# A hybrid decoder block: two VectorE operations of a recurrence step done for both heads at once, with another stage order and other buffer counts

## The chip, the cores and the metric

The kernel runs on one core of a Trainium2 chip. The core has five engines with queues of their own, which meet through semaphores: TensorE (PE in the profile; its weight loads are PEld), VectorE (DVE), ScalarE (ACT), GpSimd (POOL) and SyncE (SP), which issues most of the DMA transfers. The metric is the device time of one execution in microseconds (us).

## The reference, cut to what matters

The reference is one layer on 2048 tokens of width 1024, in float32. After an RMS norm one input projection feeds two groups of four heads, each head 128 wide. Their outputs, gated, go through one output projection and are added to the input. Then come a norm, a gated MLP (width 2816) with a causal convolution of width 3, a second addition and a last norm. The gated-DeltaNet heads carry a state matrix per head from chunk to chunk; this is the part that the change edits:

```
def step(state, inp):
    u_b, w_c, qk_c, qd_c, kd_c, cd_c = inp
    u = u_b - jnp.einsum('bhck,bhkv->bhcv', w_c, state)
    o = jnp.einsum('bhck,bhkv->bhcv', qd_c, state) + jnp.einsum('bhij,bhjv->bhiv', qk_c, u)
    state = state * cd_c[..., None, None] + jnp.einsum('bhck,bhcv->bhkv', kd_c, u)
    return state, o
```

The other four heads are retention heads: the same kind of recurrence with a fixed decay per head and rotary queries and keys.

## The kernel before

**Numbers.** Every large product is done in three passes of matmuls on split operands: each value is a high part (a rounded copy made by ScalarE) and a low part (the rest, by VectorE). `mm3` at L111 to L113 issues the three passes for channel-major and output products, L383 to L385 for token-major projections. The large products use seven multiplications in place of eight, on sums and differences of the quarters of their operands.

**Stages.** `mixers` covers everything up to the second norm, `mlp_up` the up projection and the convolution, `mlp_down` the down projection and the last norm. `mixers` works on four token blocks of 512 tokens (four chunks of 128). For each block there are items: `pro` (load and normalize x), `k0 v0 q0 kq` (retention projections, with a rotary turn L732 to L737 half on VectorE, half on GpSimd), `dec` (decays), `a0` to `a3` (one gated-DeltaNet head each: projections, convolution, transposes, Gram products), `b0 b1` (for a pair of heads, the triangular solve), `g0 g1` (the rest of the solve and the recurrence of a pair), `h0` to `h3` (retention heads), `p0 p1` (the gate projections, whose SiLU at L396 writes tiles called `mix`), `G0 G1` (gate the heads' outputs and transpose them), `W1` to `W7` (the seven products of the output projection) and `N` (residual and second norm).

**What sets the order.** The string `ORDER` names the items of all four blocks by hand, as `2k0` for item `k0` of block 2. Within it a list scheduler sets each engine's final order, interleaving the steps of several items, and each engine then runs its list strictly in order. SyncE's list holds the DMA issues, and one that must wait for its buffer holds up those behind it.

**Buffers.** On-chip tiles are slots of one size, 4 KB in each partition. A tag (`mix`, `NT`, `wvr` and so on) has an upper count in `BUFS` or in one of the N... constants, but the slots themselves are shared between tags, and the program as built fixes which slot a tile gets. So a tile can come to wait for the last reader of a quite different tile. The eight PSUM banks are shared in the same manner.

**The solve (L591 to L617).** For a pair of heads GpSimd runs 31 steps of two operations each, L603 (multiply rows of `Nb`, which a DMA brings in) and L605 (add to the rows below), about 28 us in all. Its queue also holds the rotary additions (L737), the subtractions on output-projection weights (L177) and small powers for norms (L533, L716, L812, L859).

**The recurrence (L665 to L706).** `gdn_rec` handles one chunk of a pair of heads. TensorE computes the products with the state (`ks`, L679), VectorE corrects the values (L682), TensorE applies the solved triangle (`wps`, L690), VectorE multiplies its rows by a number per row, `brk`, into `u` (L694, one operation per head), TensorE makes the state's increment and the intra-chunk output (`sps`, L698), VectorE updates the state (L700) and adds the two parts of the output (L703, one per head), and ScalarE sums the output's squares (L705). The next chunk's L679 needs the state of L700, so the four chunks of a pair are a chain; other items' matmuls fill TensorE between its links. `brk` comes from `gdn_kq` and `ss`, the squares' sums of L523, and is a small tile per head.

**Output-projection weights (L154 to L199).** `load_v` brings two halves of a weight into `wvr` tiles, GpSimd forms the needed difference in a `wvt` tile (L177; product 4 takes three subtractions per weight), ScalarE makes the high part (L197) and VectorE the low part (L198) of the `wv` tile that TensorE reads. Before the next product, `done` (L855 to L860) stores finished rows and norms them, with a power on GpSimd at L859.

**MLP constants.** `NHH` counts residual tiles and `NVV` value tiles in `mlp_down`, `NACC` the convolution's accumulators in `mlp_up`.

Of the kernel before, what the change touches and what calls it, by code (L numbers as in the profile page):

```python
# [11 lines left out]
ALU = mybir.AluOpType  # L12
# [2 lines left out]

NW = 5
LA = 1
NHH = 3
NUU = 10
NVR = 4  # L20
NVV = 20
NWUR = 2
NST = 4
NUC = 7
NACC = 6
NWU = 9
NWV = 5
FX = 1
# [5 lines left out]
NLATE = 4  # L34
NXR = 7
FD = 4
BUFS = {"n1": 8, "ykq": 5, "kv": 4, "NT": 5, "AT": 6, "o": 2, "n2s": 11, "xk": 2, "og": 1, "co": 6, "Cw": 4,
        "wx": 1, "wsq": 3, "wvr": 3, "wvt": 8, "ca": 8, "mix": 6, "D": 8, "rk": 5, "rq": 4, "rv": 8, "Ar": 1,
        "Nb": 6, "rot": 1, "rrow": 7}

ORDER = ("0pro 0k0 0v0 0dec 0a0 0q0 0a1 0a2 0h0 0b0 0h1 0a3 0b1 0g0 0kq 0g1 0h2 0p1 1pro 0p0 1k0 0G0 0h3 "
# [5 lines left out]
P = 128  # L47
S = 2048
D = 1024
# [3 lines left out]
NT = TB // P  # L53
# [149 lines left out]
def mixers(ctx, tc, base, base_used, marks, drp, mm3, gamma, mhalf, n1w, n2w, gcw, gv127, epsr, gnw, n2d, hd,  # L203
           x, xT, w_kq, w_v, w_g, w_rk, w_r0, w_r, w_o, rows, masks, rot):
    nc = tc.nc
    PE, ACT, DVE, POOL = nc.tensor, nc.scalar, nc.vector, nc.gpsimd
# [113 lines left out]
    def small(nm, n=16, bufs=2):  # L320
        if nm not in ring:
            ring[nm] = [pc(bufs, n), 0, bufs]
        e = ring[nm]
        e[1] += 1
        return e[0][:, e[1] % e[2]]
# [13 lines left out]
    def A_items(b, st):  # L339
# [165 lines left out]
        def gdn_kq(h):  # L505
            def f(w):
                hd_ = st["hd", h] = {}
                ykq = hd_["ykq"] = al("ykq", (P, 2, TB))
                ss = hd_["ss"] = small("sskq", 8, 12)
                pst = []  # L510
                for i in range(2):
                    ps = chmajor(w, i)
# [4 lines left out]
                    ps = mbank("kqtr")  # L517
# [5 lines left out]
                        ACT.activation(jk, ps[:, c * P:(c + 1) * P], AF.Square,  # L523
                                       accum_out=ss[:, i * 4 + c:i * 4 + c + 1])
                DVE.tensor_scalar(ss, ss, EPS, None, op0=ALU.add)
                brk = hd_["brk"] = small("brk", 4, 8)
                nbrk = hd_["nbrk"] = small("nbrk", 4, 8)
                bh = st["beta"].rearrange("p (t h) -> p h t", h=NH)[:, h]
                DVE.reciprocal(brk, ss[:, :4])
# [5 lines left out]
                ps = pst[0]  # L535
# [8 lines left out]
                for cc in range(2):  # L544
                    ps = mbank("kk")
                    for c1 in range(2):
                        c = cc * 2 + c1
# [117 lines left out]
        def gdn_rec(hs, c):  # L665
            def f(_):
# [8 lines left out]
                n = len(hs)  # L675
# [9 lines left out]
                    ACT.activation(e["o"][:, sl], ps[:, (n + i) * P:(n + i + 1) * P], AF.Copy,  # L685
                                   scale=st["eg"][:, jj[i]:jj[i] + 1])
                ps = rbank("wps")
                us = []
                for i, e in enumerate(H):
                    PE.matmul(ps[:, i * P:(i + 1) * P], e["TT"][:, sl], e["vp"][:, sl], start=True, stop=True)  # L690
                for i, e in enumerate(H):
                    u = small("u", P, 4)
                    us.append(u)
                    DVE.tensor_scalar(u, ps[:, i * P:(i + 1) * P], e["brk"][:, c:c + 1], None, op0=ALU.mult)  # L694
                ps = rbank("sps")
                for k, w in enumerate(("kd", "A")):
                    for i, e in enumerate(H):
                        PE.matmul(ps[:, (k * n + i) * P:(k * n + i + 1) * P], e[w][:, sl], us[i], start=True, stop=True)  # L698
                for i, h in enumerate(hs):
                    DVE.scalar_tensor_tensor(Sst[h], Sst[h], st["eg"][:, 16 + jj[i]:17 + jj[i]], ps[:, i * P:(i + 1) * P],  # L700
                                             op0=ALU.mult, op1=ALU.add)
                for i, e in enumerate(H):
                    DVE.tensor_tensor(e["o"][:, sl], ps[:, (n + i) * P:(n + i + 1) * P], e["o"][:, sl], op=ALU.add)  # L703
                    jk = small("jk", P, 1)
                    ACT.activation(jk, e["o"][:, sl], AF.Square, accum_out=e["so"][:, c:c + 1])  # L705
            return f  # L706
# [572 lines left out]
```

## Time and profile before

| | |
|---|---|
| median of three runs | 2495.29 us (2495.28 to 2497.01) |
| the profiled execution | 2495.6 us |
| its span in the trace | 2493.8 us |
| mean granted TensorE clock | 0.993 |
| busy PE, VectorE, ScalarE, GpSimd | 2413.2, 1622.6, 1000.8, 574.4 us |

The profile shows one execution, in microseconds from the start of its span. A row of a timeline gives start, duration, engine, line, operation, output and inputs, size and count; what stands in brackets is how long the engine had been idle and what released it. A row of waits gives the waiting and the releasing line, then total, count and longest. A row of windows gives busy times by engine in a stretch, the clock that TensorE was granted there (1.00 is full), the busy share of the DMA engines and GB/s. In the summary, a row of digits gives tenths for 40 equal slices of the span. Ends of matmuls are modelled, so starts are the safer reading. The mixers fill about the first 1165 us, the up projection the time to about 1960, the down projection the rest.

### The profile page before, as it was taken

Reading aid. Unit: us, or ns where it says so; the run is one execution under the profiler, and the core shown is the slowest. Engines: PE = TensorE matmul, PEld = TensorE weight load, DVE = VectorE, ACT = ScalarE, POOL = GpSimd, SP = SyncE. Lnnn points to the kernel's source line nnn. Section 1 sums busy time; section 2 is a strip of 40 time slices with the busy share of each in tenths; the row PEclk is TensorE's granted clock in tenths of the full one; section 3 lists DMA queues with packets and bytes.
Section 4 is the critical chain, followed back from the end, with each engine's and each line's share of the span. In section 5 each row is a group of like instructions: output and inputs, shape, how many; then the busy total and the mean of one; then the engine's idle time right before and its main releaser. Section 6 shows DMA issues by size and latency. Waiting matters only on the chain.

```text
span 2493.8 us, 35729 instructions
## 1 busy us (share of the span) xinstructions
PE 2413.2 (97%) x12476; PEld 2019.8 (81%) x12476; DVE 1622.6 (65%) x3198; ACT 1000.8 (40%) x2151; POOL 574.4 (23%) x891
## 2 busy tenths in 40 slices
PE   8998899999999999998899999999999999999998
PEld 7877787887888878886688888888888888888887
DVE  6755766435652673536889888896565567555795
ACT  6544544434342552425464344442222224332332
POOL 1354146521046205140011000000000001422180
PEclk9999899999999999999999999999999999999999
DMA  8756498863865646644899888867676868764794
GB/s 321 254 187 245 172 320 299 294 218 121 290 217 162 216 175 228 235 166 140 331 338 347 303 296 297 297 257 279 224 259 236 288 235 278 223 216 143 242 295 133
DMA packets 285604, 609.64 MB, mean 244 GB/s; under 512 B 40880, under 2 KB 120944, under 8 KB 285424
## 3 DMA queue, kind: packets, MB, share of 16 engines
q1 hardware_dynamic: 269424, 593.69, 67.7%
q10 hardware_dynamic: 16000, 13.67, 1.8%
q8 instruction: 98, 1.61, 0.3%
q14 instruction: 82, 0.67, 0.1%
HBM read 410.56 MB, written 196.71 MB: 244 GB/s over the span
## 4 chain that ended last, share of the span: by engine, by line
PE 78%; POOL 6%; DMA 6%; DVE 5%; issue 3%; ACT 2%; SPq 0%; ACTq 0%; POOLq 0%; DVEq 0%
PE p L111 10%; PE p L112 10%; PE p L113 10%; PE d L113 5%; PE d L111 4%; PE d L112 4%; PE tok L383 4%; PE tok L385 4%; PE tok L384 4%; PE chm L111 2%; PE chm L113 2%; PE chm L112 2%; POOL pers L605 2%; POOL pers L603 2%; DMA wvr<-in_w_o 2%
## 5 line engine op out<-in xcount | busy, mean ns | idle before, releaser
L112 PE MATMUL p<-x,wu 128*128 128x512 f32 x1176 | 458.5, 390 | 5.8 <-DVE x L929 5.8
L111 PE MATMUL p<-x,wu 128*128 128x512 f32 x1176 | 453.8, 390 | 4.6 <-ACT x L928 3.0
L113 PE MATMUL p<-x,wu 128*128 128x512 f32 x1176 | 450.6, 389 | 0.0
L383 PE MATMUL tok<-wc,n 128*128 128x512 f32 (+2 forms) x768 | 274.8, 362 | 10.8 <-ACT n L371 10.2
L384 PE MATMUL tok<-wc,n 128*128 128x512 f32 (+2 forms) x768 | 275.8, 359 | 0.0
L385 PE MATMUL tok<-wc,n 128*128 128x512 f32 (+2 forms) x768 | 274.8, 361 | 0.0
L111 PEld LDWEIGHTS p<-x,wu 128*128 128x128 f32 x1176 | 220.6, 188 | 54.5 <-ACT x L928 6.1
L112 PEld LDWEIGHTS p<-x,wu 128*128 128x128 f32 x1176 | 220.8, 188 | 54.3 <-DVE x L929 9.0
L113 PEld LDWEIGHTS p<-x,wu 128*128 128x128 f32 x1176 | 220.7, 188 | 45.3
L1049 DVE SCALAR_TENSOR_TENSOR acc<-uc,base,acc 128x1022 f32<-128x1022 f32 (+1 forms) x176 | 221.2, 1279 | 40.0 <-ACT acc L1046 34.3
L1007 DVE TENSOR_TENSOR uc<-p,uc 128x512 f32<-128x512 f32 x224 | 153.3, 687 | 133.2 <-PE p L113 131.0
L177 POOL TENSOR_TENSOR vt<-vr 128x512 f32<-128x512 f32 x44 | 70.8, 1615 | 620.5 <-DMA vr<-in_w_d 444.4
L112 PE MATMUL d<-v,uu 128*128 128x512 f32 x448 | 174.3, 389 | 0.0
L113 PE MATMUL d<-v,uu 128*128 128x512 f32 x448 | 174.3, 389 | 0.0
L111 PE MATMUL d<-v,uu 128*128 128x512 f32 x448 | 174.3, 389 | 0.0
L383 PEld LDWEIGHTS tok<-wc,n 128*128 128x128 f32 x768 | 145.9, 190 | 30.4 <-ACT n L371 10.2
L384 PEld LDWEIGHTS tok<-wc,n 128*128 128x128 f32 x768 | 145.7, 190 | 19.4
L385 PEld LDWEIGHTS tok<-wc,n 128*128 128x128 f32 x768 | 144.7, 189 | 19.3
L111 PE MATMUL chm<-n,wc 128*128 128x512 f32 x384 | 151.5, 395 | 0.0
L113 PE MATMUL chm<-n,wc 128*128 128x512 f32 x384 | 151.5, 395 | 0.0
L112 PE MATMUL chm<-n,wc 128*128 128x512 f32 x384 | 151.3, 394 | 0.0
L1054 POOL COPY base<-uc 128x2 f32<-128x2 f32 x44 | 33.2, 754 | 452.9 <-DVE uc L1007 452.9
(247 smaller groups left out, 4864.3 us busy)
## 6 DMA issues: line engine op xcount, KB each, us to landing
wu<-wu SPq DMA_DIRECT2D x308, 512.0 KB, 6.0
wc<-wd SPq DMA_DIRECT2D x166, 512.0 KB, 5.1
wv<-wo SPq DMA_DIRECT2D x84, 512.0 KB, 5.4
wd<-wc SPq DMA_DIRECT2D x60, 512.0 KB, 4.6
ur<-au SPq DMA_DIRECT2D x56, 512.0 KB, 5.5
wur<-in_w_u SPq DMA_DIRECT2D x44, 512.0 KB, 6.0
au<-st SPq DMA_DIRECT2D x88, 256.0 KB, 4.8
vr<-in_w_d SPq DMA_DIRECT2D x44, 512.0 KB, 6.0
```

Of the source, the lines that this page charges most:

```text
L111: PE.matmul(ps, ah, bh, start=(first and i == 0), stop=False, skip_group_check=chk)
L112: PE.matmul(ps, ah, bl, start=False, stop=False, skip_group_check=chk)
L113: PE.matmul(ps, al, bh, start=False, stop=(i == n - 1), skip_group_check=chk)
L177: POOL.tensor_tensor(tt[:, j], a, b_, op=ALU.subtract)
L383: PE.matmul(ps, ah, wh, start=(k == 0), stop=False)
L384: PE.matmul(ps, ah, wl, start=False, stop=False)
L385: PE.matmul(ps, al_, wh, start=False, stop=(k == KT - 1))
L603: POOL.tensor_tensor(tm[:, :, :n], Nb[:, j:j + 1, j + 1:].to_broadcast([P, 8, n]), X[:, :, j:j + 1].to_broadcast([P, 8, n]), op=ALU.mult)
L605: POOL.tensor_tensor(X[:, :, j + 1:], X[:, :, j + 1:], tm[:, :, :n], op=ALU.add)
L1007: add = lambda o, ps, a: DVE.tensor_tensor(o, ps, a, op=ALU.add)
L1049: DVE.scalar_tensor_tensor(acc[:, t:], u[:, :T2 - t], w, acc[:, t:], op0=ALU.mult, op1=ALU.add)
L1054: POOL.tensor_copy(mhalo[:, ci], u[:, T2 - 2:])
```

## The change

In `gdn_rec` the two scalings into `u` become one VectorE multiplication over both heads, 128 partitions by 2 by 128, with the row factors broadcast along the last axis. For that, the factors of a pair are put side by side in one small tile. The tile `u` holds both heads, with two buffers in place of four of half the size. The two output additions become one over both heads, which works because the heads of a pair already share one output tile. The matmuls and ScalarE's squares are as before.

In `ORDER`, `1h3` and `2k0` change places, as do `2v0` and `2dec`; `2p1` and `2p0` come right after `1N`, ahead of `3pro`; in block 3 `h0` and `h1` change places, and `3b1` moves from ahead of `3kq` to behind `2W4`. Five buffer counts rise: NHH 3 to 5, NVV 20 to 22, NACC 6 to 7, NT 5 to 6, mix 6 to 8.

```diff
-NHH = 3
+NHH = 5
-NVV = 20
+NVV = 22
-NACC = 6
+NACC = 7
...
-BUFS = {"n1": 8, "ykq": 5, "kv": 4, "NT": 5, ... "ca": 8, "mix": 6, "D": 8, ...
+BUFS = {"n1": 8, "ykq": 5, "kv": 4, "NT": 6, ... "ca": 8, "mix": 8, "D": 8, ...
...
-         "1p1 1h2 1p0 1g1 1h3 2k0 1G0 1G1 2v0 2dec 1W1 1W2 2a0 1W6 1W7 1W5 1W3 2a2 2a1 2b0 2q0 1W4 2h1 "
-         "2a3 2b1 2h0 2g0 2g1 1N 3pro 2p1 2kq 2h2 2p0 2G0 3k0 2h3 2G1 3dec 3a0 2W1 2W2 3a1 2W6 3v0 3b0 "
-         "3q0 3h1 2W7 2W5 3a2 2W3 3h0 3a3 3b1 3kq 3p0 3g0 3h2 2W4 3g1 3G0 2N 3p1 3h3 3G1 3W1 3W2 3W6 3W7 "
+         "1p1 1h2 1p0 1g1 2k0 1h3 1G0 1G1 2dec 2v0 1W1 1W2 2a0 1W6 1W7 1W5 1W3 2a2 2a1 2b0 2q0 1W4 2h1 "
+         "2a3 2b1 2h0 2g0 2g1 1N 2p1 2p0 3pro 2kq 2h2 2G0 3k0 2h3 2G1 3dec 3a0 2W1 2W2 3a1 2W6 3v0 3b0 "
+         "3q0 3h0 2W7 2W5 3a2 2W3 3h1 3a3 3kq 3p0 3g0 3h2 2W4 3b1 3g1 3G0 2N 3p1 3h3 3G1 3W1 3W2 3W6 3W7 "
...
-                brk = hd_["brk"] = small("brk", 4, 8)
+                if ("brk", h // 2) not in st:
+                    st["brk", h // 2] = small("brk", 8, 5)
+                brk = hd_["brk"] = st["brk", h // 2][:, h % 2 * NT:(h % 2 + 1) * NT]
...
-                us = []
...
-                for i, e in enumerate(H):
-                    u = small("u", P, 4)
-                    us.append(u)
-                    DVE.tensor_scalar(u, ps[:, i * P:(i + 1) * P], e["brk"][:, c:c + 1], None, op0=ALU.mult)
+                h2 = lambda t: t.rearrange("p (i d) -> p i d", i=n)
+                u = small("u", n * P, 2)
+                DVE.tensor_tensor(h2(u), h2(ps[:, :n * P]),
+                                  h2(st["brk", hs[0] // 2])[:, :, c:c + 1].to_broadcast([P, n, P]), op=ALU.mult)
...
-                        PE.matmul(ps[:, (k * n + i) * P:(k * n + i + 1) * P], e[w][:, sl], us[i], start=True, stop=True)
+                        PE.matmul(ps[:, (k * n + i) * P:(k * n + i + 1) * P], e[w][:, sl], u[:, i * P:(i + 1) * P], start=True, stop=True)
...
+                op = st["op", hs[0] // 2][:, :, sl]
+                DVE.tensor_tensor(op, h2(ps[:, n * P:]), op, op=ALU.add)
                 for i, e in enumerate(H):
-                    DVE.tensor_tensor(e["o"][:, sl], ps[:, (n + i) * P:(n + i + 1) * P], e["o"][:, sl], op=ALU.add)
                     jk = small("jk", P, 1)
                     ACT.activation(jk, e["o"][:, sl], AF.Square, accum_out=e["so"][:, c:c + 1])
```

More of the change, by code (lines that the diff above doesn't have):

```diff
@@ L36 @@
 FD = 4
-BUFS = {"n1": 8, "ykq": 5, "kv": 4, "NT": 5, "AT": 6, "o": 2, "n2s": 11, "xk": 2, "og": 1, "co": 6, "Cw": 4,
-        "wx": 1, "wsq": 3, "wvr": 3, "wvt": 8, "ca": 8, "mix": 6, "D": 8, "rk": 5, "rq": 4, "rv": 8, "Ar": 1,
+BUFS = {"n1": 8, "ykq": 5, "kv": 4, "NT": 6, "AT": 6, "o": 2, "n2s": 11, "xk": 2, "og": 1, "co": 6, "Cw": 4,
+        "wx": 1, "wsq": 3, "wvr": 3, "wvt": 8, "ca": 8, "mix": 8, "D": 8, "rk": 5, "rq": 4, "rv": 8, "Ar": 1,
         "Nb": 6, "rot": 1, "rrow": 7}
```

## The prediction

> **What bounds the kernel now.** I read the page's engine shares first, then the PE waits summed by line, then windows and the order of time around the longest waits.
>
> ```profile
> span 2493.8 us, 35729 instructions
> PE 2413.2 (97%) x12476; PEld 2019.8 (81%) x12476; DVE 1622.6 (65%) x3198; ACT 1000.8 (40%) x2151; POOL 574.4 (23%) x891
> ...
> PEclk9999899999999999999999999999999999999999
> PE wo L111 <- ACT wv L197: 6.3, 3, 4.5
> PE sps L698 <- DVE pers L694: 5.8, 11, 0.7
> ...
> PE ks L679 <- ACT mix L396: 5.7, 1, 5.7
> ...
> PE vtr L569 <- ACT pers L523: 2.3, 1, 2.3
> ...
> PE d L113 <- DVE u L1128: 1.4, 2, 0.8
> ```
>
> TensorE is busy in 97% of the span, VectorE in 65%, so the two operations that are merged lie on an engine with spare time. No matmul is added or taken away. What can change is the time in which PE waits or runs slowly, and the waits are all short: the line that the change edits, L694, ends 5.8 us of PE waiting in 11 cases, half a microsecond each. The PEclk row has eights only within the first 450 us, the first two token blocks; the rest of the kernel has little to give back or to lose.
>
> The largest avoidable piece is in block 1, where product 4 of the output projection needs its second weight.
>
> ```profile
> 431.23 1.05 PE L794 MATMUL rkk<-ykq 128*128 128x128 f32 x8
> 432.04 0.48 PE L112 MATMUL chm<-n,wc 128*128 128x512 f32 x1
> ...
> 432.81 0.39 PE L112 MATMUL chm<-n,wc 128*128 128x512 f32 x1
> 433.04 0.39 PE L113 MATMUL chm<-n,wc 128*128 128x512 f32 x1
> 437.95 1.22 PE L111 MATMUL wo<-wv,wu 128*128 128x512 f32 x2 [4.52 <-ACT wv L197]
> ...
> 442.81 0.63 PE L113 MATMUL chm<-n,wc 128*128 128x512 f32 x1
> 443.23 0.48 PE L111 MATMUL chm<-n,wc 128*128 128x512 f32 x1
> 437.27 0.63 ACT L197 ACTIVATE wv<-wvt 128x512 fp32r<-128x512 f32 x1 [2.02 <-POOL wvt L177]
> 435.46 0.55 POOL L859 TENSOR_TENSOR pers<-pers,base 128x1 f32<-128x1 f32 x1
> 435.98 1.25 POOL L177 TENSOR_TENSOR wvt<-wvr,wvt 128x512 f32<-128x512 f32 x1
> 433.20:436.60 3.40, 0.23 (x2) 0.00 (x0) 0.00 (x0) 1.15 (x1) 3.40 (x7) 1.00 1.03 417
> 436.60:440.00 3.40, 2.05 (x5) 1.67 (x6) 1.91 (x2) 1.78 (x2) 3.40 (x5) 0.50 0.49 198
> 440.00:443.40 3.40, 3.40 (x10) 2.63 (x9) 0.67 (x1) 0.63 (x1) 3.17 (x7) 0.50 0.97 290
> ```
>
> The columns of the last three rows are the stretch, its length, the busy time of PE, weight load, VectorE, ScalarE and GpSimd, and the granted clock. PE stops at 433.43 and starts again at 437.95: 4.5 us. The wait goes back through ScalarE's high part (437.27) to GpSimd's last subtraction (435.98), which stands in GpSimd's queue among the solve of the first head pair and behind the two L859 powers. Then the clock is 0.50 for 6.8 us. Wide matmuls then start 0.42 us apart (442.81, 443.23) instead of 0.23 (432.81, 433.04): twelve of them fill 437.95 to 443.23, so 5.28 minus 12 x 0.23, 2.5 us, is lost on top. Together 7.0 us. Eight narrow ones take 0.81 (431.23 to 432.04), 0.10 each.
>
> **The merged operations.** Thirty-two chunk steps (4 blocks, 2 pairs, 4 chunks) each lose one scaling and one addition on VectorE.
>
> ```profile
> L694 DVE TENSOR_SCALAR pers<-wps,pers 128x128 f32<-128x128 f32 x64 | 19.4, 345 | 35.4 <-PE wps L690 35.3
> ...
> L703 DVE TENSOR_TENSOR o<-sps,o 128x128 f32<-128x128 f32 x64 | 15.4, 283 | 0.0
> ...
> L424 DVE TENSOR_TENSOR co<-og,co 128x256 f32<-128x256 f32 x16 | 6.7, 422 | 7.8 <-ACT co L423 6.3 <-PE ks L679 0.9 <-ACT og L423 0.6
> 1153.45 0.61 DVE L694 TENSOR_SCALAR pers<-wps,pers 128x128 f32<-128x128 f32 x2 [0.58 <-PE wps L690]
> ...
> 1153.86 0.75 PE L698 MATMUL sps<-pers,kv 128*128 128x128 f32 x4 [0.44 <-DVE pers L694]
> ...
> 1154.44 0.61 PE L698 MATMUL sps<-pers,AT 128*128 128x128 f32 x4
> 1155.09 0.60 DVE L700 SCALAR_TENSOR_TENSOR pers<-pers,pers,sps 128x128 f32<-128x128 f32 x2 [1.03 <-PE sps L698]
> ...
> 1155.61 0.48 DVE L703 TENSOR_TENSOR o<-sps,o 128x128 f32<-128x128 f32 x2
> ```
>
> A merged operation has 256 columns instead of 128. The trace has none of that width that reads PSUM, so I bound it: below by one old L694, 0.34 us, above by two back to back, 0.61. I take 0.42, from L424, which has that width and two tensors, in SBUF. VectorE's busy time falls by 64 x 0.345 + 64 x 0.283 - 64 x 0.42 = 13 us, on an engine that is not the bound. The timeline rows show a chunk with nothing beside it, the only place where the saving can reach PE. L694 twice takes 0.61 us from 1153.45; the state products start 0.41 after that, and the A products, which need nothing more than the second scaled row, 0.58 later, where four narrow ones need 0.45: 0.13 lost. Merged, the state products start 0.42 - 0.34 = 0.08 later and the 0.13 goes: 0.05 gained per bare chunk, 0.5 us for the 11 waits of L694. Bounds: 11 x 0.13 = 1.4 gained at 0.34, 11 x (0.27 - 0.13) = 1.5 lost at 0.61. The merged addition takes 0.42 against 0.48 for two, but the first head's square on ScalarE starts 0.42 - 0.28 = 0.14 later; that matters only behind a pair's last chunk (8 places, 1.1 us at most), and L700, which releases the next chunk, stands ahead of it either way. Together -0.5, between -1.4 and +2.6. The shared reciprocal tile adds no instruction.
>
> **Stage order, block 1.** Here I compare the two programs' orders on each engine, where positions can be read without times. The four subtractions' place on GpSimd changes most. Before, the second weight's last subtraction comes some 24 iterations into the 31-iteration solve; after, it comes in the fourth, since its load is issued well ahead. It no longer has the L859 powers ahead of it. So the 4.5 us wait goes and with it the half clock, 7.0 us.
>
> What is late next is the third and the fourth weight. Their loads need buffers that product 3 frees, and are issued once its last matmul is done; call that t.
>
> ```profile
> wvr<-in_w_o SPq DMA_DIRECT2D x5, 512.0 KB, 7.1
> ```
>
> A load takes 7.1 us here (median from issue to landing, five of them) and a subtraction 1.25. Third weight: issued at t + 0.5, landed at 7.6, three subtractions with the solve's steps of 0.4 between them, done at 12.4, ScalarE's half at 13. Its first matmul comes 68 instructions after t, at 13.6 (16 narrow at 0.10, 52 wide at 0.23): 0.6 in hand. The retention product's decayed tile, L795, now takes over the buffer of the fourth weight's load and waits for the first subtraction that reads it, at 13.6; behind it on VectorE stands the third weight's low part. It ends at 14.3 and is wanted at 14.3: nothing in hand. Fourth weight: its second load waits for the third weight's first subtraction (9.0), lands at 16.1, two subtractions to 19.0, ScalarE to 19.5, wanted at 18.8. Behind other issues on SP all three come later by as much. I give back 1.5 us, so the place is worth -5.5, between -7.0 and 0. GpSimd's solve itself waits at the L859 powers and ends about 8 us later; the first matmul that wants it stands 288 instructions behind product 3's last, 192 of them wide (44 us), so other work covers it. Without that cover, it would cost up to those 8.
>
> ```profile
> 403.99 0.39 PE L384 MATMUL tok<-wc,n 128*128 128x512 f32 x1
> 406.69 0.66 PE L569 MATMUL vtr<-base,ca 128*128 128x128 f32 x4 [2.32 <-ACT pers L523]
> ```
>
> The value transposes waited 2.3 us for ScalarE's squares, with 21 projection matmuls ahead. The new order puts 30 and two wide ones there and the four Gram products behind. Nine more at 0.23 cover 2.0: -2.0, between -2.3 and 0.
>
> **Stage order, blocks 0, 2 and 3.**
>
> ```profile
> 217.74 1.57 ACT L396 ACTIVATE mix<-tok,pers 128x256 f32<-128x256 f32 x4 [9.53 <-POOL pers L603]
> 265.90:269.30 3.40, 1.82 (x16) 1.63 (x16) 1.07 (x6) 3.37 (x7) 0.04 (x1) 1.00 0.04 17
> 269.30:272.70 3.40, 3.17 (x15) 2.68 (x15) 1.74 (x9) 1.17 (x4) 0.00 (x0) 0.50 0.01 2
> ...
> 286.40:289.80 3.40, 3.40 (x15) 3.08 (x16) 3.33 (x15) 2.00 (x8) 1.01 (x1) 0.50 0.00 0
> ...
> 146.43:149.84 3.41, 1.70 (x10) 1.15 (x9) 0.00 (x0) 0.00 (x0) 2.66 (x10) 1.00 0.13 52
> 149.84:153.26 3.42, 1.66 (x15) 1.69 (x16) 1.94 (x5) 0.73 (x1) 1.74 (x5) 1.00 0.38 72
> ```
>
> In block 0 the gate's tile still gets the buffer that the second pair's solve reads to its end, so ScalarE's 9.53 us wait and PE's 5.7 us stay. What changes is which matmuls stand in front: fifteen projection matmuls come before the next state read, which is 15 x 0.23 = 3.4 us later in the chain of pair 1, while other work comes between the bare chunks at the end. I take 0. Bounds: 3.4 lost if nothing of it is covered; 6.2 gained if the 12.5 us of PE work that ran at 0.50 in this tail (3.17 in the second row, 3.40 in the fourth, and two windows between) ran at full clock.
>
> ```profile
> 802.70 0.22 POOL L605 TENSOR_TENSOR pers<-pers 128x8 f32<-128x8 f32 x1
> 804.39 0.48 PE L384 MATMUL tok<-wc,n 128*128 128x512 f32 x1
> ```
>
> In block 2 both gates now come before the next block's normalization. One gate tile takes the buffer of the second pair's solve, whose last operation ran at 802.7; the tile's own matmuls stand behind the state products, where L384 ran at 804.4, so a margin of about 2 us hides it. Swapping block 3's retention heads and moving its second solve to behind product 4 leave the bare chunks and the solve's position on GpSimd as they are. Every moved load keeps its distance on SP to within a few issues. I take 0 for both, between -0.7 and +1.9.
>
> **Buffer counts.** NHH, NVV and NACC act on the two MLP stages. PE waits there on VectorE's L1128 for 1.4 us in all; more value buffers let those loads start earlier. I take -0.7, half of it, between -1.4 and 0. NT and mix only widen which slots may be handed out; their effect is in the order above.
>
> **The sum**, against the profiled execution's 2495.6 us (0.3 over the median of the runs shown, 2495.29): -0.5 - 5.5 - 2.0 + 0 + 0 - 0.7 = -8.7, so 2486.9.
>
> **A rule beside the rows.** The row of 265.9 to 269.3 shows 1.82 us of PE work in 3.4, and the clock is 0.50 in the next; that of 146.43 shows 1.70 and the next, 149.84, has the full clock, so busy time alone does not decide. The Trainium skill, TensorE: Matmul & The Clock Gate, Part 1, says the clock halves after an idle window of about 3.4 us on a free-running grid. The wait at 433 agrees (0.23 us busy in one window, then 0.50); the tail of block 0 does not, for no window there is idle. By the rule, a longer tail in block 0 would cost its waits alone, 3.4 us at most and 2490.3 in all; by the rows it costs the clock too, as in the first rival. Since the row contradicts the rule here, I give its version 0.03 of that rival's chance.
>
> **The rivals.**
> First: block 0's tail gets longer. For it speaks the state read pushed back by 3.4 us; against it the better mixed rest. Price 3.4, and two more windows at half clock, 1.7 each: 6.8. Time 2493.7, within 0.2%. It outweighs the rest from 8.7 us on.
> Second: the order gives nothing, because the third and the fourth weight wait as long as the second did. For it: margins of 0.6 and 0.0 us. Against: the same subtractions, fewer of them late. Then only the merge, the transposes and the buffers remain: -3.2, 2492.4.
> Third, slower: those loads are late twice over. Two loads in series stand between product 3 and the fourth weight, in a stretch where the DMA share is 1.03 (row of 433.2). If each takes 12 us instead of 7.1, PE waits 0.7 + 2 x 4.9 = 10.5, and three windows at half clock cost 1.7 each, 5.1: 15.6 against the 7.0 that go, so +8.6 - 3.2 = +5.4 and 2501.0. It cancels the gain once the waits there reach about 10 us with their clock, with two windows (0.7 + 2 x 3.0 + 3.4), that is from loads of some 10 us on. Against it: the five loads of this stretch have a median of 7.1.
>
> **How the numbers follow.** Forecast 0.53; first rival 0.18; second 0.12; third, with any other buffer handed to a late reader at that price, 0.17. A change of 0.2% (5 us) is about what can be told from none. Faster: 0.53 and a share of the first two, 0.55; same 0.27; slower 0.18. The low end is the sum with most of its good bounds (-1.4 - 7.0 - 2.3 - 1.4 = -12.1, and 5.0 of the 6.2 in block 0): 2478.5. The high end is the third rival, 2501. The forecast's own range is 2479 to 2490.
>
> **What would show it.** L694 and L703's successors: 32 each at about 0.42 us. No PE wait over 1 us on the output projection between 420 and 450, clock 1.00 there. The value transposes of block 1 without their 2.3 us. Clock rows of 0.50 in block 0 as long as before. It is wrong if the block-1 weights' wait is still several microseconds, if the half-clock stretches in the first 300 us grow, or if a new wait of a gate tile for the solve appears near 800.

## The result, and the profile after

The changed kernel takes 2503.16 us in the median of seven runs (2500.12 to 2505.14); the kernel before took 2495.29 beside it (seven runs, 2492.72 to 2497.68). The ratio is 1.0029, with a 95% interval of 1.0017 to 1.0041: slower by 0.3%, where 0.3% faster was forecast. The profiled execution took 2505.1 us, 9.2 us more in its span than the one before (2503.0 against 2493.8).

The summary rows of the changed kernel, and its groups for the two merged operations (busy time, mean duration in ns, idle time before them):

```profile
span 2503.0 us, 35747 instructions
...
PE 2419.4 (97%) x12476; PEld 2023.0 (81%) x12476; DVE 1607.6 (64%) x3134; ACT 1003.6 (40%) x2151; POOL 571.4 (23%) x891
```

```profile
L694 DVE TENSOR_TENSOR pers<-wps,pers 128x256 f32<-128x256 f32 x32 | 13.5, 422 | 40.3 <-PE wps L691 40.2
...
L704 DVE TENSOR_TENSOR o<-sps,o 128x256 f32<-128x256 f32 x32 | 13.4, 417 | 0.0
```

The merged operations take what they were costed at: 32 of each kind, 0.42 us each. VectorE's busy time is down by 15.0 us, of which 7.9 belong to these two operations (19.4 + 15.4 us in the prediction's rows, 13.5 + 13.4 here); the rest lies in other operations. PE has 6.2 us more busy time for the same matmuls: they run longer at half clock (mean clock 0.991 against 0.993).

The next rows are, of the changed kernel, the windows of the stretch in which product 4 of block 1 waited before and of the end of the down projection (length, busy PE, weight load, VectorE, ScalarE, GpSimd, clock, DMA share, GB/s), and PE's waits by line and releaser (total, times, longest). The down projection's matmuls start at 2062 us in the kernel before, not at about 1960 as said ahead of the prediction:

```profile
400.00:450.00 50.00, 48.73 (x241) 40.35 (x240) 23.36 (x54) 23.87 (x71) 41.75 (x63) 1.00 0.89 312
...
2355.00:2380.00 25.00, 25.00 (x112) 20.71 (x111) 18.41 (x22) 7.88 (x14) 12.34 (x8) 1.00 0.96 319
2380.00:2405.00 25.00, 25.00 (x112) 20.71 (x111) 23.51 (x22) 9.80 (x17) 24.07 (x16) 1.00 1.01 302
2405.00:2425.00 20.00, 19.84 (x88) 16.07 (x87) 17.26 (x19) 6.58 (x13) 16.45 (x10) 1.00 1.00 323
2425.00:2450.00 25.00, 20.23 (x77) 15.56 (x76) 21.68 (x26) 10.29 (x17) 10.99 (x10) 0.86 0.68 204
```

```profile
PE tok L383 <- DVE rq L736: 2.9, 1, 2.9
...
PE d L113 <- DVE u L1130: 3.1, 2, 2.9
PE d L111 <- ACT v L197: 1.6, 1, 1.6
PE d L112 <- DVE v L198: 0.2, 1, 0.2
```

The same windows of the kernel before:

```profile
400.00:450.00 50.00, 43.16 (x201) 35.60 (x200) 23.36 (x42) 18.61 (x51) 45.72 (x74) 0.93 0.84 297
...
2355.00:2380.00 25.00, 25.00 (x112) 20.67 (x111) 23.73 (x24) 8.90 (x18) 16.39 (x11) 1.00 0.99 322
...
2425.00:2450.00 25.00, 24.41 (x106) 19.42 (x106) 20.18 (x28) 9.75 (x18) 8.54 (x8) 1.00 0.67 200
```

The 4.5 us wait of block 1 is gone with its half clock: 48.7 us of PE work in the 50 us from 400, against 43.2. But there are two new places: PE waits 2.9 us near 486 for VectorE's rotary queries, and 4.9 us in the down projection, where 25 us now hold 20.2 us of PE work at a mean clock of 0.86, against 24.4 at 1.00.

To see where the 9.2 us come from, PE's work is summed in each trace (each matmul counted at the median spacing of its kind in the kernel before, 0.227 us for 512 columns), and the times are compared at which the same amount is done. Up to 199 us and from 1301 us on, both kernels issue the same matmuls in the same order; there the numbers are exact, being differences of one matmul's start. In between they are estimates from these spacings. Less the kernel before, by the time of the latter, for the changed kernel and for the first run below, which has the old two counts of the down projection (us):

| at | 137 | 166 | 375 | 427 | 460 | 511 | 624 | 938 | 1165 | 2321 | end |
|---|---|---|---|---|---|---|---|---|---|---|---|
| changed | +0.7 | +3.2 | +1.2 | -1.3 | -6.7 | -1.5 | +0.2 | +2.4 | +2.3 | +3.1 | +9.2 |
| changed, old MLP counts | +0.5 | +0.3 | -1.4 | -3.9 | -9.5 | -5.8 | -7.5 | -7.5 | -7.6 | -6.8 | -6.9 |

So three things stand out: 5.4 us gained between 427 and 460, which is the block-1 wait; 5.2 us given back by 511; 6.1 us lost at the end, behind 2321. The 2.5 us at 150 are a clock matter, told in the last section.

### The profile page after: what moved, and what is told of

The parts are those of the page before. It is cut to its first block, busy times and chain, and to the rows that moved or that the text cites. A ratio compares the mean times of both kernels' runs of the same rounds, so it can differ in the third digit from the quotient of the medians.

```text
span 2503.0 us, 35747 instructions
## 1 busy us (share of the span) xinstructions
PE 2419.4 (97%) x12476; PEld 2023.0 (81%) x12476; DVE 1607.6 (64%) x3134; ACT 1003.6 (40%) x2151; POOL 571.4 (23%) x891
## 5 line engine op out<-in xcount | busy, mean ns | idle before, releaser
L383 PE MATMUL tok<-wc,n 128*128 128x512 f32 (+2 forms) x768 | 275.9, 363 | 20.4 <-ACT n L371 10.6
L1051 DVE SCALAR_TENSOR_TENSOR acc<-uc,base,acc 128x1023 f32<-128x1023 f32 (+1 forms) x176 | 221.0, 1279 | 41.7 <-ACT acc L1048 41.7
L383 PEld LDWEIGHTS tok<-wc,n 128*128 128x128 f32 x768 | 147.0, 192 | 40.5 <-ACT n L371 10.6
```

Of the source, the lines that this page charges most:

```text
L383: PE.matmul(ps, ah, wh, start=(k == 0), stop=False)
L1051: DVE.scalar_tensor_tensor(acc[:, t:], u[:, :T2 - t], w, acc[:, t:], op0=ALU.mult, op1=ALU.add)
```

## The experiments

All times are medians against the kernel before, run beside it; the interval is that of the ratio.

**The MLP counts taken back.** The changed kernel with the old two counts of the down projection:

```diff
-NHH = 5
+NHH = 3
-NVV = 22
+NVV = 20
```

> The changed kernel with NHH back at 3 and NVV at 20, everything else as changed. On every engine its order is that of the changed kernel up to the down projection. Theory A (the two counts reorder the down projection's loads, and the stall near 2433 and its half clock come from that): the time falls by about 8.6 us, from 2503 to 2494 to 2495, and the PE waits on L1130 and on L197 there fall to under 1.5 us in all. Theory B (the down projection is only hit because the mixers' work reaches it at another moment or clock phase): no change, 2500 to 2505, with the same 3 us wait.

Measured: 2494.86 (11 runs, 2488.71 to 2497.8) against 2495.1, ratio 0.9997 (0.9988 to 1.0005). The whole loss goes with these two counts, and what is left of the change is worth nothing that can be told, not the 8.0 us that the other terms promised. The profiled execution was the fastest of the eleven, with a span of 2486.9: there part of the block-1 gain is kept (second row of the table), and the down projection loses nothing.

**The MLP counts alone,** in the kernel before, both and one at a time:

```diff
-NHH = 3
+NHH = 5
-NVV = 20
+NVV = 22
```

> The kernel before with NHH 5 and NVV 22 alone. Theory A: slower by about 8 us, 2503, nothing changed before 2350 us, and a PE wait of about 3 us near 2430 followed by 6.8 us at half clock. Theory B: as before, 2494 to 2497.

> The kernel before with NHH 5 alone. Theory D (the residual tiles: with five of them the residual loads go out earlier and push the last product's weight loads back): most of the loss, 2500 to 2503, with a PE wait of 2 to 3 us near 2430. Theory E (the value tiles: with 22 of them all eleven weights of a product can be brought in ahead): same as before, 2494 to 2497. Either way TensorE's order and everything ahead of 2000 us is that of before.

> The kernel before with NVV 22 alone. Theory E: 2500 to 2503, with the wait near 2430. Theory D: 2494 to 2497. If each shows half, the two add up.

Measured: both 2502.03 (1.0026, 1.0015 to 1.0037); NHH alone 2501.38 (1.0032, 1.0019 to 1.0046); NVV alone 2502.59 (1.0034, 1.0022 to 1.0045). Each count alone costs what both cost, so the costs don't add up, and theories D and E each foretold one of the two. On PE all three issue the matmuls of the kernel before in the same order; their waits in the down projection sum to 4.4, 4.4 and 5.3 us, against 1.4. Either count changes when the loads go out, and what hangs on them.

**The merge alone and the order alone,** in the kernel before (the `gdn_rec` part of the diff with its shared `brk` tile; the new `ORDER` string):

> The kernel before with the merged scaling and the merged addition alone (old ORDER, old counts). Theory A says that the mixers as a whole gain nothing: block 1's weight wait (4.5 us and half clock, 7.0) goes but is given back by 500 us, because a rotary product there waits for GpSimd; by the trace of the changed kernel the merge's part is -2 to +2 us, 2493 to 2497. Theory C (the stage order, not the merge, moved block 1, as the prediction had it): block 1 keeps the 4.5 us wait at 433, and the time is within 1 us of before because VectorE is not the bound.

> The kernel before with the new ORDER alone. Its order on TensorE is that of before up to the 3847th instruction, in block 2, so block 1's weight wait at 433 must stay. Theory A: 2494 to 2497, the 0.9 us wait at 812 replaced by one of similar size near 852. Theory C: 7 us faster, 2488, without the wait at 433.

Measured: merge 2498.14 (11 runs; 1.0015, 1.0006 to 1.0024), which is 3.0 us slower and 1 us outside the range foretold; order 2496.54 (11 runs; 1.0007, 0.9998 to 1.0016). PE's waits between 100 and 600 us, in the merge alone and then in the order alone:

```profile
PE tok L383 <- ACT mix L396: 5.4, 1, 5.4
...
PE tok L383 <- DVE rq L736: 3.9, 1, 3.9
```

```profile
PE ks L679 <- ACT mix L396: 5.7, 1, 5.7
PE wo L111 <- DMA hd<-Cw: 4.3, 1, 4.3
...
PE vtr L569 <- ACT pers L523: 2.3, 1, 2.3
```

With the merge alone, product 4's wait is gone and the wait of 3.9 us for the rotary queries is there. With the order alone, PE still waits 4.3 us on the output projection and 2.3 us at the value transposes, a wait that the merge alone removes (0.2 us are left). So the block-1 rearrangement does not come from the `ORDER` string: with the merged operations the list scheduler came to another interleaving, on PE from block 0's first recurrence on and on GpSimd from block 1 on.

**The merged addition alone.**

```diff
-    DVE.tensor_tensor(e["o"][:, sl], ps[:, (n + i) * P:(n + i + 1) * P], e["o"][:, sl], op=ALU.add)
+op = st["op", hs[0] // 2][:, :, sl]
+DVE.tensor_tensor(op, ps[:, n * P:2 * n * P].rearrange("p (i d) -> p i d", i=n), op, op=ALU.add)
```

> The kernel before with the merged output addition alone. Its order stays nearly that of before: on GpSimd for the first 630 instructions (into block 3), on SyncE for 474. Theory H (a merged operation by itself is worth almost nothing, since VectorE is not the bound): 2494 to 2497, block 1 with its 4.5 us wait at 433, VectorE's busy time 4.7 us less (64 x 0.283 - 32 x 0.42). Theory I (VectorE's queue matters): 2 to 3 us faster.

Measured: 2494.81 (1.0001, 0.9991 to 1.001), with the waits of the kernel before in block 1 (2.7 us for ScalarE's `wv`, 2.0 at the value transposes). The merged addition costs nothing and brings nothing.

**More room for the rotary products.** The 486 us wait goes through `rt`, a ring of two small tiles that GpSimd's addition frees. With the old MLP counts:

```diff
-                tt = small("rt", P, 2)
+                tt = small("rt", P, 4)
```

> The changed kernel with NHH 3 and NVV 20 and, beside that, four buffers instead of two for the rotary products that VectorE hands to GpSimd. Theory F (block 1's gain is given back because VectorE's third rotary product waits for GpSimd, which is still in the solve): without that wait the mixers keep 3 to 5 us of it, 2489 to 2492. The planner writes a new order for this, from the first block on; if that matters more than the wait (theory G), the time can be anything from 2489 to 2500 and the rest of the trace, not the wait, explains it.

Measured: 2504.97 (9 runs, 2498.84 to 2518.17; 1.0049, 1.0032 to 1.0065). The wait near 486 fell only to 1.5 us, and the scheduler came to another order from block 0 on, with new waits in several places (2.1 us at 937 among them). It tells nothing on the ring itself.

**One subtraction off GpSimd.** In the changed kernel the very last weight's third subtraction stands behind a column's power (L1137) on GpSimd, in the kernel before ahead of it. I took that for the cause and moved this one instruction; all others keep their order on their engines. (`down` stands for the test that the weight is one of the down projection's.)

```diff
-            src = sub(0, qs[2], src)
+            src = sub(0, qs[2], src, DVE if k == NP - 1 and down else POOL)
```

> The changed kernel with one instruction moved: the third subtraction of the down projection's very last weight runs on VectorE instead of GpSimd, so that it no longer stands behind a column's power in GpSimd's queue. All other instructions keep their engines and their order on PE, ScalarE and SP. Theory J (the order on GpSimd's queue is the loss): no PE wait over 1.2 us and no half clock between 2425 and 2450, the 8.6 us go, median 2494 to 2496, as with the old counts. Theory K (more buffers let loads and subtractions run earlier and crowd VectorE; the place of the one subtraction is incidental): the waits of the down projection stay at 4 us or more with their half clock, median 2500 to 2504.

**And eight rotary additions off GpSimd.** The same, and in block 1 the first two row tiles of `kq` add on VectorE:

```diff
-                rotate(t, ps[:, :256], dk)
-                rotate(t, ps[:, 256:], dq)
+                rotate(t, ps[:, :256], dk, DVE if b == 1 and t < 2 else POOL)
+                rotate(t, ps[:, 256:], dq, DVE if b == 1 and t < 2 else POOL)
```

> As the kernel before it in this call, and besides the rotary additions of retention pair 1 for the first two row tiles of block 1 (eight instructions of 0.45 us) run on VectorE instead of GpSimd. The order of the instructions is the same up to block 1's end and again from there. Theory L (block 1's gain was given back because these additions queue behind the second solve on GpSimd): the PE wait of 3.1 us near 486 falls below 1 us, its half clock goes too, and the median is 3 to 5 us under that of the kernel before it, about 2489 to 2492. Theory M (another reader of the late solve waits in its place): a wait of 2 us or more turns up between 480 and 560, and the median is within 1.5 us of the kernel before it.

**All subtractions of the last product off GpSimd.** The changed kernel with the 33 of them on VectorE:

```diff
+        eng = DVE if i == 4 and down else POOL
-        src = sub(0, qs[1], qs[0])
+        src = sub(0, qs[1], qs[0], eng)
```

(and the other two in the same way)

> The changed kernel with all 33 subtractions of the down projection's last product on VectorE. Theory N (two-tensor work of VectorE and GpSimd slows each other down): between 2355 and 2432 VectorE's 1024-wide splits take about 1.2 us as they do when GpSimd is idle, instead of 2.3 beside subtractions, so that VectorE carries the 33 subtractions of about 0.7 us each (23 us) without being busy longer than 85 % of that stretch, and no PE wait over 1.2 us remains in the down projection: median 2494 to 2496. Rival (VectorE is slow there of itself): the splits stay over 1.8 us, VectorE falls behind by 20 us and PE waits 5 us or more: median 2504 or over.

Measured, against 2494.46: one subtraction 2499.43 (12 runs; 1.0021, 1.001 to 1.0032); with the rotary additions 2496.39 (11 runs; 1.0004, 0.9994 to 1.0014); all subtractions 2490.63 (11 runs; 0.9982, 0.9972 to 0.9991).

Theory J fell. With the one subtraction moved, PE still waits in the down projection and the half clock is there, as its waits and a window show:

```profile
PE d L113 <- DVE u L1130: 3.5, 2, 2.9
PE d L112 <- DVE v L198: 0.9, 1, 0.9
```

```profile
2425.00:2450.00 25.00, 21.23 (x80) 16.20 (x79) 21.36 (x28) 10.64 (x20) 8.04 (x7) 0.86 0.69 202
```

Theory L held: near 486 no wait for rotary queries is left, the clock there is 1.00, and the time is 3.0 us under its neighbour, though the two intervals overlap and the median did not come down to the 2489 to 2492 foretold. That run and these rows show the chain. They are of GpSimd, VectorE and PE, first of the changed kernel's timeline, then of the kernel before:

```profile
474.27 0.62 POOL L605 TENSOR_TENSOR pers<-Nb,pers 128x248 f32<-128x248 f32 x1 [10.16 <-DMA Nb<-z]
...
486.22 1.02 POOL L814 TENSOR_TENSOR pers<-pers,base 128x4 f32<-128x4 f32 x1
487.21 0.45 POOL L739 TENSOR_TENSOR rk<-rk,pers 128x128 f32<-128x128 f32 x1
487.69 0.29 DVE L734 TENSOR_TENSOR pers<-tok,rot 128x128 f32<-128x128 f32 x1 [5.67 <-POOL rk L739]
...
488.77 0.28 DVE L736 TENSOR_TENSOR rq<-tok,rot 128x128 f32<-128x128 f32 x1
489.10 0.80 PE L383 MATMUL tok<-wc,n 128*128 128x512 f32 x1 [2.93 <-DVE rq L736]
```

```profile
479.37 0.62 POOL L603 TENSOR_TENSOR pers<-Nb,pers 128x248 f32<-128x248 f32 x1 [12.99 <-DMA Nb<-z]
...
492.21 0.88 POOL L737 TENSOR_TENSOR rk<-rk,pers 128x128 f32<-128x128 f32 x2
493.33 0.28 DVE L734 TENSOR_TENSOR rq<-tok,rot 128x128 f32<-128x128 f32 x1
492.02 0.48 PE L383 MATMUL tok<-wc,n 128*128 128x512 f32 x1
```

GpSimd could start block 1's second solve only at 474.27, when the DMA of `Nb` had landed; the rotary additions stand behind 18 of its operations in the queue and start at 487.21. VectorE can't write the next rotary product until then (5.67 us idle), the projection's PSUM bank stays full, and PE waits. In the kernel before the queue is much the same, and all of it is 5 us later (479.37, 492.21), so GpSimd kept most of PE's lead of 6.1 us. What is new is the dependence: there the same matmul, the first of its projection, started at 492.02, ahead of the rotary query of 493.33 and without a wait; in the changed kernel it starts right behind that query's end. That the changed program gives it another PSUM bank is inferred from these times and not shown by a run.

Theory N held in the main. VectorE's groups of the changed kernel between 2355 and 2430, then GpSimd's, then those of the kernel with all subtractions on VectorE, with its windows:

```profile
L1130 DVE TENSOR_TENSOR uu<-ur,uu 128x1024 fp32r<-128x1024 f32 x10 | 14.9, 1488 | 0.2
L1138 DVE SCALAR_TENSOR_TENSOR C<-C,base,fnw 128x1024 f32<-128x1024 f32 x6 | 13.8, 2306 | 2.5 <-POOL base L1137 2.5
L1152 DVE TENSOR_TENSOR C<-d,C 128x512 f32<-128x512 f32 x10 | 6.7, 682 | 5.5 <-PE d L113 5.5
L1135 DVE TENSOR_TENSOR base<-base 128x1 f32<-128x1 f32 x6 | 5.3, 881 | 0.0
```

```profile
L177 POOL TENSOR_TENSOR vt<-vr,vt 128x512 f32<-128x512 f32 x20 | 34.0, 1700 | 4.4 <-DMA vr<-in_w_d 3.6
L177 POOL TENSOR_TENSOR vt<-vr 128x512 f32<-128x512 f32 x11 | 19.5, 1770 | 99.0 <-DMA vr<-in_w_d 99.0
```

```profile
L1131 DVE TENSOR_TENSOR uu<-ur,uu 128x1024 fp32r<-128x1024 f32 x13 | 15.7, 1218 | 1.3 <-ACT uu L1130 1.3
L177 DVE TENSOR_TENSOR vt<-vr,vt 128x512 f32<-128x512 f32 x22 | 14.9, 684 | 0.6 <-DMA vr<-in_w_d 0.6
L1139 DVE SCALAR_TENSOR_TENSOR C<-C,base,fnw 128x1024 f32<-128x1024 f32 x8 | 10.2, 1278 | 1.9 <-POOL base L1138 1.9
...
L1153 DVE TENSOR_TENSOR C<-d,C 128x512 f32<-128x512 f32 x11 | 7.4, 682 | 0.0
...
L1136 DVE TENSOR_TENSOR base<-base 128x1 f32<-128x1 f32 x8 | 1.2, 151 | 0.4 <-ACT jk L1144 0.4
```

```profile
2355.00:2380.00 25.00, 25.00 (x112) 20.71 (x111) 21.20 (x33) 10.80 (x18) 0.93 (x1) 1.00 1.03 327
2380.00:2405.00 25.00, 25.00 (x112) 20.71 (x111) 25.00 (x41) 10.57 (x19) 2.94 (x3) 1.00 1.05 362
2405.00:2425.00 20.00, 20.00 (x90) 16.57 (x89) 17.78 (x30) 8.33 (x15) 2.07 (x3) 1.00 0.98 311
2425.00:2450.00 25.00, 25.00 (x112) 20.68 (x111) 13.27 (x21) 6.96 (x15) 2.19 (x4) 1.00 0.53 165
```

Beside GpSimd's subtractions a 1024-wide scaling of two SBUF tensors (L1138) takes 2.31 us, without them 1.28; the split of 1024 columns (L1130) takes 1.49, without them 1.22; an addition of 128x1 takes 0.88 instead of 0.15; the accumulation that reads one operand from PSUM (L1152) takes 0.68 both times. A subtraction takes 1.70 to 1.77 us on GpSimd and 0.68 on VectorE. So VectorE does 33 operations more and is busy 77.3 us of the 95 from 2355 to 2450 (21.20 + 25.00 + 17.78 + 13.27), against 80.9 in the changed kernel (18.41, 23.51, 17.26, 21.68 in the same windows). Over the same 410 matmuls, where the changed kernel is 6.8 us behind, it is 77.4 against 84.4. It is still 90% busy from 2355 to 2432, where at most 85% was foretold, yet no wait of PE is recorded there any more. The Trainium skill, SBUF — State Buffer, section Who interferes with whom, says that a VectorE instruction with two SBUF inputs and a GpSimd instruction that reads SBUF lock each other out for a whole instruction, and that a VectorE instruction with at most one SBUF input, outside its two-port modes, doesn't contend; these rows agree in which operations are longer (L1130, L1138 and the 128x1 addition, not L1152).

**Loads earlier, GpSimd kept.** Two tries to bring the last product's weights earlier with the larger counts:

```diff
-            want = min(NP, (tp + 1) * 2)
+            want = min(NP, (tp + 1) * 2 + 1)
```

> The changed kernel with the down projection's next weights asked for one column of work earlier (one more weight ahead), counts and engines as they are. Theory Q (the larger counts let other loads go ahead of the last product's weights on SP's queue, so that the last weight comes 5 to 8 us later and its subtractions with it): the last of these loads is issued at least 5 us earlier against PE's work, no PE wait over 1.2 us and no half clock between 2400 and 2450, median 2494 to 2496. Rival R (VectorE is crowded by GpSimd whenever the weights come): waits of 3 us or more stay in the down projection, median 2499 to 2504.

```diff
-NVR = 4
+NVR = 5
```

> The changed kernel with five buffers for the raw weight quarters of the down projection instead of four, so that the last product's loads stand about five places earlier on SP's queue; all subtractions stay on GpSimd. Theory Q (late loads make the loss): the last of these loads is issued at 2418 us of PE's work or earlier (2422.4 in the changed kernel, 2414.9 before), the waits of the down projection sum to 2 us or less without half clock, median 2493.5 to 2497. Rival R (VectorE is crowded by GpSimd whenever the weights come): waits of 3 us or more and the half clock stay, median 2499 to 2505.

Measured: 2505.54 (6 runs; 1.0042, 1.0028 to 1.0055) and 2502.36 (6 runs, 2495.86 to 2508.7; 1.0032, 1.002 to 1.0045). Where the last weight load is issued, put on PE's scale (its time less PE's lag to the kernel before at 2321 us, the difference in start of the same matmul), and PE's waits for operands from 2330 to 2450:

| kernel | issued | PE's lag | on PE's scale | waits |
|---|---|---|---|---|
| before | 2414.9 | 0 | 2414.9 | 1.4 |
| changed, old MLP counts | 2408.0 | -6.8 | 2414.8 | 1.3 |
| changed, raw ring of 5 | 2409.2 | -4.1 | 2413.3 | 3.8 |
| changed | 2423.7 | +3.1 | 2420.7 | 4.9 |
| changed, one subtraction moved | 2420.8 | -0.6 | 2421.4 | 4.4 |
| changed, one weight ahead | 2425.1 | +0.2 | 2424.9 | 7.2 |
| changed, all subtractions on VectorE | 2407.8 | -3.7 | 2411.5 | 0 |

The first try did the opposite of its edit: the load came later, and so did not test theory Q. The second, whose waits and windows follow, brought it 7.4 us forward, ahead even of its place in the kernel before (the 2422.4 in the expectation is 2420.7 by the table). Yet the largest wait only moved: 2.0 us at 2403 instead of 2.9 at 2433, with a shorter stretch of half clock (0.91 over 20 us). It also waits 2.5 us at 2097, where its last matmuls of the up projection and its first of the down projection come in another order.

```profile
PE d L113 <- DVE u L1130: 3.8, 3, 2.0
```

```profile
2380.00:2405.00 25.00, 23.50 (x104) 19.14 (x102) 23.76 (x20) 8.66 (x16) 23.23 (x14) 1.00 0.93 306
2405.00:2425.00 20.00, 18.18 (x72) 14.55 (x73) 17.32 (x19) 7.01 (x12) 14.43 (x12) 0.91 0.66 205
```

So theory Q fell and rival R holds: with the last load 1.6 us ahead of its old place, 3.8 us of waits stay, with the half clock. A late last load is not needed for the loss. A VectorE crowded by GpSimd is not enough for it either: over the same 410 matmuls VectorE is busy 84.0 us in the kernel before, where PE waits 1.4 us, and 84.4 in the changed one. The loss takes both, the loads as the larger counts place them and the subtractions on GpSimd. Which feature of the new placing does it is open: on PE's scale the second half of the 22 loads comes 0.3 to 5.8 us later than before in the changed kernel, and up to 5.7 us earlier in nearly all cases with the ring of five.

**Both repairs, and the control.** The changed kernel with all 33 subtractions and the eight rotary additions on VectorE; and the kernel before with the 33 subtractions alone.

> The changed kernel with both repairs: all 33 subtractions of the down projection's last product on VectorE, and the eight rotary additions of block 1 on VectorE. If the two losses are separate, the repairs add: 3 us under the first alone (2490.6), 2486.5 to 2488.5, and the waits at 486 and in the down projection are both gone. If the block-1 gain is still given back elsewhere, 2490 to 2492.

> The kernel before with the 33 subtractions of the down projection's last product on VectorE, nothing else. If e11's time under the kernel before is the changed kernel's order (the block-1 wait that goes), this stays within 1 us of the kernel before less its two waits there (0.9 and 0.8 us): 2492.5 to 2494.5. If the moved subtractions alone make e11 faster, it falls to 2491 or under.

Measured, against 2494.98: both repairs 2489.26 (12 runs; 0.9979, 0.9969 to 0.9989), the control 2492.46 (12 runs; 0.9991, 0.9982 to 0.9999). Both repairs together have the lowest median of the study, 0.2% under the kernel before. The wait in the down projection is gone, and of that at 486 there are 1.2 us left, now of a state read that VectorE's rotary query releases. The second repair's 3 us didn't add: 1.4 us by medians, with overlapping intervals, between the two forecasts. Of the 5.7 us, 2.5 belong to the moved subtractions alone, which lies at the edge of the first forecast; the remaining 3.2 are what the rest of the change is worth together with the moved rotary additions, though the two intervals overlap. The traces speak more plainly than the times: the eight with a larger count and all or all but one of the subtractions on GpSimd have a half clock between 2380 and 2450, the nine others have 1.00 throughout.

## Why the prediction was wrong

**The merged operations: right in size, wrong in effect.** 0.42 us each, as costed. The 13 us saved on VectorE were added up from mean durations, though two old operations overlap (0.61 us for two of 0.345); by the groups' busy times it is 7.9. The small gain of 0.5 us on PE wasn't seen: PE's waits for L694 are 7.1 us in 12 cases, against 5.8 in 11. Alone, the merge costs 3.0 us (interval 1.5 to 6), where at most 2.6 were allowed for, and the merged addition alone nothing. What the part missed is that the merge acts through the scheduler.

**Stage order, block 1: the mechanism was right, its cover was not.** The wait and its half clock went, and with them 5.4 us (from -1.3 to -6.7 in the table), where -5.5 was forecast; weights 3 and 4 cost one wait of 1.1 us for VectorE's low part. Two steps failed. First the cause: it is the merge that moves the subtractions, not `ORDER`, as the two single runs show. Second the cover: "GpSimd's solve ... ends about 8 us later; ... other work covers it". I priced the solve's own reader, 288 instructions on, and left out what is queued behind the solve on GpSimd. The rotary additions stand there, and they hold VectorE, a PSUM bank and, in the new order, PE. The wait of 2.9 us and its half clock return the gain within 30 us: PE's lead of 6.1 us at 485 is 1.5 at 511.

**The value transposes: right, by another cause.** The 2.3 us are gone, and the table moves by 2.5 between 375 and 427; but the merge does it, not the stage order.

**Blocks 0, 2 and 3: right in the main.** Blocks 2 and 3, taken as 0 with at most +1.9, move by +2.1 between 624 and 1165 in the changed kernel's trace and by -0.1 in that of the same program with the old MLP counts. Block 0's gate still waits (5.4 us at L383 in the merge alone, 5.5 in the changed kernel), no gate waits for a solve near 800, and the first rival's longer tail did not come.

**Buffer counts: the step that failed, by about 8 us.** "More value buffers let those loads start earlier", -0.7. They started later, and the term is +6.1 us in the changed kernel's trace and 6.9 to 8.2 by the medians of the counts alone. SyncE's issues in the kernel before and in the changed one:

```profile
2347.54 1.10 SPq L169 DMA_DIRECT2D vr<-in_w_d  x1
2351.73 3.74 SPq L1145 DMA_DIRECT2D hh<-hd  x3
```

```profile
2347.54 4.94 SPq L1147 DMA_DIRECT2D hh<-hd  x3
...
2354.80 2.00 SPq L1147 DMA_DIRECT2D hh<-hd  x3
...
2357.85 0.33 SPq L169 DMA_DIRECT2D vr<-in_w_d  x1
```

The first load of the last product's weights was issued at 2347.54 before and at 2357.85 after, 7.2 us later on PE's scale, since with more residual buffers five more residual loads (L1147) go ahead of it on the one queue; the last load comes 5.8 us later. With NVV alone the first load keeps its place and the last one comes 5.5 us later (issued at 2418.87, PE 1.6 us ahead); why that count moves it was not tried. The same 33 subtractions on GpSimd then meet VectorE's last columns at another moment. Earlier loads would not have helped by themselves: with the ring of five most of the later ones are early, and the kernel is as slow. I had the row that showed how little room was there, VectorE 65% busy over the whole span, and did not read it by stage: it is 23.7 us of 25 from 2355 in the kernel before. An average over the span hid a stretch where VectorE is nearly the bound.

The third rival had the right sign and almost the time (2501.0), by luck: it put the late loads in block 1, where none were.

## What to carry to other kernels

A deeper buffer can let its own loads go ahead, as the residual tiles did here, and on an in-order queue that means that other loads go behind; look at what they feed, in the stage where it lies. For an engine off the critical path read the busy share by stage, and treat two-operand SBUF work on VectorE and GpSimd at the same time as one resource: moving the GpSimd half to VectorE made VectorE less busy here. When a wait is removed, ask for each in-order queue what else stands behind the work that PE is to overtake and which buffers it holds, not only who reads that work. And where a scheduler sets the order, compare the schedules after every edit: the merge moved more than the stage order did.

## What the runs showed of the hardware

**The clock follows more than the stall.** The same stall can cost its own time alone or several us more. PE waits 3.3 to 3.5 us at 148 us in the kernel before, in the changed one and in the one with the old MLP counts; these windows are of the three in that order:

```profile
150.00:160.00 10.00, 8.40 (x49) 7.46 (x50) 5.77 (x13) 4.53 (x12) 2.25 (x6) 1.00 0.63 182
```

```profile
150.00:160.00 10.00, 7.87 (x34) 7.17 (x35) 5.77 (x13) 2.40 (x4) 2.62 (x8) 0.66 0.61 182
```

```profile
150.00:160.00 10.00, 8.09 (x48) 7.19 (x49) 5.77 (x13) 4.71 (x13) 2.47 (x7) 1.00 0.62 182
```

Only the second fell to half clock, and the second and the third are the same program up to the down projection. In the 5 us from 145 PE was busy 3.13, 3.80 and 3.62 us, so that the busiest of the three fell. Of all 17 traces, five kept the full clock there. At 486 us a wait of 2.1 us left the clock at 1.00 with the old MLP counts, and one of 2.4 us brought half clock with one subtraction moved. This may be a part of why executions of one program lie 9 us and more apart (2488.71 to 2497.8 with the old counts, 2487.72 to 2500.59 for 25 of the kernel before), and a single trace can show a gain that the median doesn't have. The Trainium skill, TensorE: Matmul & The Clock Gate, Part 1, lets the clock halve after an idle window of 3.4 us on a free-running grid. A grid that runs free would explain why the same stall falls differently each time, which no run here shows; that the window must be idle does not fit, for ahead of the half clock in the down projection the longest idle stretch is 2.9 us.

**Blocked time is shown as busy time.** A 128x1 addition of 0.15 us is recorded with 0.88 us on average beside GpSimd's subtractions. VectorE's busy time rises beside them, so it overstates the work that is there to be moved.
